# Attention over memory tokens: key loads moved from GpSimd's queue to SyncE's, with slots apart from the values

## The chip, the cores and the metric

The kernel runs on one core of one Trainium2 chip. The metric is device time in microseconds (us) of one execution, lower is better. The engines are named as in the profile: PE is TensorE (matmuls), PEld its weight loads, DVE is VectorE, ACT is ScalarE, POOL is GpSimd, SP is SyncE, which only issues DMAs. PSUM is where matmuls accumulate; SBUF is the on-chip memory from which engines read; DRAM holds inputs, outputs and scratch.

## The reference, cut to what matters

One decoder layer is computed for a prompt (256 tokens) and for 8 samples of 8 tokens (64 tokens), with the same weights: a mixer (state space and short convolution), attention over 256 memory tokens, and a retrieval layer over single-neuron experts (PEER). The change lies in the attention, 4 heads of 512:

```python
def mem_attend(xn, k, v, wq, wo):
    b, L, _ = xn.shape
    q = (xn @ wq).reshape(b, L, MEM_HEADS, MEM_HEAD_DIM)
    s = jnp.einsum('blhd,bmhd->bhlm', q, k.astype(q.dtype)).astype(jnp.float32) * (1.0 / math.sqrt(MEM_HEAD_DIM))
    p = jax.nn.softmax(s, axis=-1)
    o = jnp.einsum('bhlm,bmhd->blhd', p.astype(v.dtype), v).reshape(b, L, D_MODEL)
    return (o @ wo).astype(xn.dtype)
```

For the samples, keys and values are inputs (`cache_mem_k`, `cache_mem_v`), one set for each sample and head. For the prompt they are computed at the start of the kernel, written out as results (`p_mem_k`, `p_mem_v`), and read back here. A tile is the keys, or the values, of one sample (or of the prompt) for one head: 256 tokens x 512 numbers in fp32, 512 KB, held as 128 partitions x 1024. That makes 4 heads x (8 samples + 1 prompt) = 36 key tiles and 36 value tiles.

## The kernel before, in words

All of the work is one stream of units (class `Stream`). A unit has up to four parts: `load` (asks for a weight tile by DMA), `first` (for a key tile: the transpose on DVE, L1363), `second` (split of an fp32 tile into a high part H on ACT, L248, and a low part L on DVE, L249), and `comp` (the matmuls). `add` puts a unit into the stream; its `first` runs in program order some units later (`ahead`), and its `comp` later still, when more units of its kind are queued than `room` allows. So the code itself writes down the order of PE, ACT and DVE (`MANUAL` names these three engines). The order of requests on SP and on POOL isn't fixed by hand there: the framework's planner sorts each of these queues while it builds the program, and puts a wait ahead of each request for the slot that it fills. Later in the kernel POOL's order is fixed too, but not in the stage of the change.

In the attention stage three kinds of units alternate (list `steps`): weight units of the next head's query projection (`panel`, `w_mem_q`) or of the output projection (`w_mem_o`), key units and value units. Weight tiles (W) are 512 KB each, in four slots, asked for by SP. Key units of head h come nine to a head: eight samples, then the prompt. Value units of a head follow its keys by nine key steps and four more (`nk`, `LAG`), so that the values of head h run between the keys of head h+1; after the last key only values and weight units are left.

Key units of samples: `next_tile()` hands out a loaded tile kv, `turned` transposes it into a tile tt (three buffers), and `comp` multiplies it with the queries into pss (L1408). From that moment, the end of the transpose, the kv slot is free. Key units of the prompt: the same transpose, then the split into H and L, then psp (L1424 to L1426). When a head's scores are complete, a side job copies them (SC, L1307), gathers them by further matmuls (psm, L1314), and runs the softmax. Value units of samples: `first` only hands out the tile, and the matmuls of two tiles run together in the second one's `comp` (pso, L1448); the slots of both are free after that. Value units of the prompt: split, then po (L1466 to L1468), then the split of the result into AH and AL.

Loads before: `kv_load` appends a closure to one list, `loads`, for keys and values in the order in which they are used, and `next_load` runs the next one. All ask on POOL's queue: two DMAs of 256 KB for a sample's keys (L1129, each fills 64 partitions), four of 128 KB for the prompt's keys (L1129, 32 partitions), one of 512 KB for values (L1132). All share ten slots of one tag (`KVT`), seven in pool KV and three in pool PQ, used in turn. Eight tiles are asked for ahead of the stage; from the fourth tile on, each `next_tile` first asks for one more (`KV_AHEAD` = 5), so that five tiles of either kind are ahead.

Of the kernel before, what the change touches and what calls it, by code (L numbers as in the profile page):

```python
# [11 lines left out]
F32 = mybir.dt.float32  # L12
# [7 lines left out]
P = 128  # L20
# [5 lines left out]
NB = 8  # L26
# [15 lines left out]
PE_U, PE_B, DVE_T, ACT_H, DVE_L, POOL_L = 1.44, 1.36, 0.66, 0.6, 0.76, 1.36  # L42

HLB, GD, WA, WB = 7, 6, 3, 4
TU, AB, TTB, KVT, KV1, OB = 5, 3, 3, 10, 7, 3

R_SSD, R_BEST, R_CHOOSE, R_CHOOSE2, R_OUT = 0.7, 0.6, 0.40, 0.32, 0.29
XW, LAG = 5, 4
# [1 line left out]
Q_AHEAD, Q_ROOM, KV_AHEAD = 5, 4, 5  # L50
# [113 lines left out]
def step(ctx, tc, ins, outs, dbg=None, stop=None):  # L164
    nc = tc.nc
# [78 lines left out]
    strm = Stream(WA, g=GD, a=2)  # L244
# [869 lines left out]
        scaled_split(h[:, k], l[:, k], x[:, k], gain(g, k))  # L1114
        add_square(nrm, acc, x[:, k], k == 0)

    loads = deque()
    ready = deque()
    tiles = count()
    PQ = {}  # L1120

    def kv_load(src, blocks):
        def load():
            own = next(tiles) % KVT < KV1
            t = (KV if own else PQ)["pool"].tile([P, 1024], F32, tag="kv", bufs=KV1 if own else KVT - KV1, name="kv")
            if blocks:
                n, p = 512 // blocks, P // blocks
                for e in range(blocks):
                    nc.gpsimd.dma_start(t[p * e:p * e + p].rearrange("p (a d) -> p a d", d=n),  # L1129
                                        src[:, n * e:n * e + n].rearrange("(a p) d -> p a d", p=p))  # L1130
            else:
                nc.gpsimd.dma_start(t.rearrange("p (m d) -> p m d", m=2), src.rearrange("(m p) d -> p m d", p=P))  # L1132
            ready.append(t)
        loads.append(load)

    def next_load():
        if loads:
            loads.popleft()()

    skipped = count()  # L1140

    def next_tile():
        if next(skipped) >= NB - KV_AHEAD:
            next_load()
        return ready.popleft()

    KV = {}

# [6 lines left out]
    for c in range(8):  # L1155
        gemm(w_out[0], 256 * c, 256, AH, AL, T, lambda m, pt, c=c: evac_next(XF, 2 * c + m, pt, norm_sum(1), 2, BH, BL))
        strm.then(lambda c=c: nc.gpsimd.dma_start(x1_d[:, 2 * c:2 * c + 2], XF[:, 2 * c:2 * c + 2]))
        if c == 1:
            strm.then(open_kv)
        if 2 <= c <= 5:  # L1160
            strm.then(next_load)
            if c < 5:
                strm.then(next_load)
    if dbg is not None and "x1" in dbg:
        strm.flush()
        dump("x1", XF)
# [7 lines left out]

    def open_q():
        PQ["pool"], PQ["close"] = pool("pQ")
        next_load()
    strm.then(open_q)

    def panel(w2d, c, ah, al, evac, wide=False, need=()):  # L1180
# [44 lines left out]
    def open_tiles():  # L1225

        pq = PQ["pool"]
        PQ["sel"] = pq.tile([P, TS], F32, name="sel")
        iv = ident.rearrange("p (y u x q) -> p y u x q", y=2, u=2, q=LS)
        V.tensor_tensor(PQ["sel"].rearrange("p (x y q) -> p y x q", y=2, q=LS), iv[:, :, 0], iv[:, :, 1], ALU.add)  # L1230
        def clear(name, shape):
            t = pq.tile(shape, F32, name=name)
            S.activation(t, ident[:, 0:shape[2]].unsqueeze(1).broadcast_to(shape), AF.Copy, scale=0.0)
            return t
        PQ["half"] = clear("half", [P, 4, 32])
        for s in range(2):
# [124 lines left out]
    def turned(t, k):  # L1361
        tt = PQ["pool"].tile([P, 1024], F32, tag="tt", bufs=TTB, name="tt")
        V.transpose(tt.rearrange("p (k a i) -> p k a i", k=k, i=32), t.rearrange("p (a k j) -> p k a j", k=k, j=32))  # L1363
        return tt

    def prompt_units(src, keys, comp):

        kv_load(src, 4 if keys else 0)
        box = {}

        def unit(u):
            def first():
                if u == 0:
                    t = next_tile()
                    box["t"] = turned(t, 4) if keys else t

            def second():
                h, l = high(), low()
                split(h, l, box["t"][:, 512 * u:512 * u + 512])
                box[u] = h, l  # L1380

            def third():
                comp(u, *box.pop(u))

            return None, first, second, third, "a"

        return [unit(0), unit(1)]

    def head(h):

        st = {}

        def sample_scores(b):

            if h:
                kv_load(cache_k[0, b, :, h], 2)

            def first():
                st["k", b] = turned(next_tile(), 8)

            def comp():
                if b == 0:
                    st["ss"] = ps("pss")
                tt = st.pop(("k", b))
                for i in range(2):
                    for j in range(4):
                        k = 4 * i + j
                        PE.matmul(st["ss"][32 * j:32 * j + 32, P * (b // 2):P * (b // 2) + P], PQ["qm"][:, k * NB + b],  # L1408
                                  tt[:, P * k:P * k + P], start=b % 2 == i == 0, stop=b % 2 == i == 1)
                if b == NB - 1:  # L1410
                    strm.side(sample_softmax(st["ss"], h), 1 + h // 3)

            return [(None, first, None, comp, "a")]

        def prompt_scores(u, kh, kl):
            if u == 0:
                st["sp"] = ps("psp")
            for j in range(2):
                c = 2 * u + j
                for qb in range(2):  # L1420
                    out = st["sp"][:, TP * qb:TP * qb + TP]
                    qh, ql = (PQ[n][:, c, qb * P:qb * P + P] for n in ("qh", "ql"))
                    k0, k1 = kh[:, TP * j:TP * j + TP], kl[:, TP * j:TP * j + TP]
                    PE.matmul(out, qh, k0, start=c == qb == 0, stop=False, skip_group_check=True)  # L1424
                    PE.matmul(out, qh, k1, start=False, stop=False, skip_group_check=True)
                    PE.matmul(out, ql, k0, start=False, stop=c == 3, skip_group_check=True)  # L1426
            if u == 1:
                strm.side(prompt_softmax(st["sp"], h), 1 + h // 3)

        def sample_values(b):  # L1430

            def unit(i):
                kv_load(cache_v[0, i, :, h], 0)

                def first():
                    st["v", i] = next_tile()

                def comp():
                    if i == b:
                        return  # L1440
                    assert ("pm", h) in done
                    if b == 0:
                        st["so"] = ps("pso")
                    vs = [st.pop(("v", n)) for n in (b, i)]
                    for y, v in enumerate(vs):
                        for u in range(2):
                            g = 2 * y + u
                            PE.matmul(st["so"][32 * g:32 * g + 32], PQ["pm"][:, u * NB + b + y], v[:, 512 * u:512 * u + 512],  # L1448
                                      start=b == 0, stop=b == NB - 2)
                    if i == NB - 1:  # L1450
                        st["res"] = strm.side(sample_result(st["so"], h), 1 + h // 2)
                        done.add(("sv", h))

                return None, first, None, comp, "a"

            return [unit(b), unit(b + 1)]

        def prompt_values(u, vh, vl):
            assert ("ph", h) in done
            if u == 0:  # L1460
                st["po"] = [ps(f"po{c}") for c in range(2)]
            for j in range(4):
                out = st["po"][j // 2][:, TP * (j % 2):TP * (j % 2) + TP]
                v0, v1 = vh[:, j * P:(j + 1) * P], vl[:, j * P:(j + 1) * P]
                p0, p1 = PQ["ph"][:, u], PQ["pl"][:, u]
                PE.matmul(out, v0, p0, start=u == 0 and j % 2 == 0, stop=False, skip_group_check=True)  # L1466
                PE.matmul(out, v0, p1, start=False, stop=False, skip_group_check=True)
                PE.matmul(out, v1, p0, start=False, stop=u == 1, skip_group_check=True)  # L1468
            if u == 1:
                for c in range(2):  # L1470
                    k = 4 * h + 2 * c
                    split(AH[:, k:k + 2, 0:TP], AL[:, k:k + 2, 0:TP], st["po"][c].rearrange("p (j t) -> p j t", t=TP))
                done.add(("pv", h))

        def keys(b):
            return sample_scores(b) if b < NB else prompt_units(p_mem_k[0, 0, :, h], True, prompt_scores)

        def values(b):
            if b == NB:
                return prompt_units(p_mem_v[0, 0, :, h], False, prompt_values)  # L1480
            return sample_values(b - 1) if b % 2 else []

        return keys, values
# [451 lines left out]
    box = {}  # L1935

    turned, lowered, used = {}, {}, {}
# [364 lines left out]
```

## Time and profile before

| what | us |
|---|---|
| median of 3 runs | 3092.66 |
| lowest and highest of them | 3091.08, 3093.04 |
| the profiled execution | 3084.24 |
| its span, first to last instruction | 3082.5 |
| PE busy in the span | 3047.4 |
| DVE, ACT, POOL busy | 2269.7, 1586.2, 1347.8 |
| first transpose of a key tile, start | 1157.8 |
| last matmuls with sample values, start | 1347.9 |

The profile is one execution on the chip. A line such as "1314.39 1.25 DVE L1363 ..." in an order of time is: start in us from the span's start, duration in us, engine, line of the kernel, operation, tile written <- tiles read (buffer numbers left out), their shapes, how many instructions in a row, and in brackets how long the engine stood before it and what ended that. An engine with a q (SPq, POOLq) is its sequencer. POOL's DMA lines show how long POOL took to issue, not to transfer. In a table by windows the columns are the window, its length, the busy us of PE, PEld, DVE, ACT and POOL with their instruction counts, the granted PE clock, the busy share of the 16 DMA engines, and GB/s. A row on waits is "who <- what it waited for: us in total, times, longest".

### The profile page before, as it was taken

Reading aid. Unit: us, or ns where it says so; the run is one execution under the profiler, and the core shown is the slowest. Engines: PE = TensorE matmul, PEld = TensorE weight load, DVE = VectorE, ACT = ScalarE, POOL = GpSimd, SP = SyncE. Lnnn points to the kernel's source line nnn. Section 1 sums busy time; section 2 is a strip of 40 time slices with the busy share of each in tenths; the row PEclk is TensorE's granted clock in tenths of the full one; section 3 lists DMA queues with packets and bytes.
Section 4 is the critical chain, followed back from the end, with each engine's and each line's share of the span. In section 5 each row is a group of like instructions: output and inputs, shape, how many; then the busy total and the mean of one; then the engine's idle time right before and its main releaser. Section 6 shows DMA issues by size and latency. Waiting matters only on the chain. (4 is left out here: it accounts for less than half of the span.)

```text
span 3082.5 us, 55315 instructions
## 1 busy us (share of the span) xinstructions
PE 3047.4 (99%) x19709; PEld 2791.6 (91%) x19709; DVE 2269.7 (74%) x4478; ACT 1586.2 (51%) x3200; POOL 1347.8 (44%) x1500
## 2 busy tenths in 40 slices
PE   8999999999999999999999999999999999999998
PEld 7889999999999999889999999888888888888886
DVE  5556866666566556656778899988885888888886
ACT  5545543434454443444454444766674555555555
POOL 0011221111110002410458999988887656455553
PEclk9999999999999999999999999999999999999999
DMA  7988899899999858975966788878998999999996
GB/s 270 294 266 301 308 332 328 307 331 308 356 327 344 296 185 225 268 246 159 239 205 222 286 320 316 303 290 323 332 333 270 351 338 364 321 348 338 319 314 216
DMA packets 445321, 909.19 MB, mean 295 GB/s; under 512 B 43336, under 2 KB 252400, under 8 KB 419572
## 3 DMA queue, kind: packets, MB, share of 16 engines
q1 hardware_dynamic: 316372, 543.31, 51.5%
q0 software_dynamic: 60656, 227.34, 22.4%
q10 hardware_dynamic: 68016, 135.01, 12.8%
q8 instruction: 154, 2.52, 0.3%
q14 instruction: 123, 1.01, 0.1%
HBM read 849.44 MB, written 190.05 MB: 337 GB/s over the span
## 5 line engine op out<-in xcount | busy, mean ns | idle before, releaser
L249 DVE TENSOR_TENSOR L<-W,H 128x512 fp32r<-128x512 f32 x1312 | 900.7, 711 | 360.7 <-ACT H L248 351.4
L248 ACT ACTIVATE H<-W 128x512 fp32r<-128x512 f32 x1312 | 796.6, 628 | 684.8 <-PE acc L2170 232.2
L1979 POOL TENSOR_TENSOR L<-tt,H 128x512 fp32r<-128x512 f32 x511 | 646.4, 1296 | 59.9 <-ACT H L1976 52.7
L371 PE MATMUL pg<-AH,H 128*128 128x320 f32 x1856 | 581.7, 313 | 0.0
L373 PE MATMUL pg<-AH,L 128*128 128x320 f32 x1856 | 573.7, 309 | 0.0
L372 PE MATMUL pg<-AL,H 128*128 128x320 f32 x1856 | 573.4, 309 | 0.0
L2169 PE MATMUL acc<-L,wt 128*128 128x512 f32 x1024 | 398.7, 389 | 1.1 <-DVE L L249 1.0
L2170 PE MATMUL acc<-H,wt 128*128 128x512 f32 x1024 | 398.4, 389 | 0.0
L2168 PE MATMUL acc<-H,wt 128*128 128x512 f32 x1024 | 398.4, 389 | 0.0
L1976 ACT ACTIVATE H<-tt 128x512 fp32r<-128x512 f32 x512 | 308.6, 625 | 144.2 <-DVE tt L1967 117.5
L1967 DVE STREAM_TRANSPOSE tt<-W 128x512 f32<-128x512 f32 x512 | 337.6, 690 | 56.9 <-POOL L L1979 52.7
L1998 PE MATMUL pu<-XP,H 128*128 128x512 f32 x1035 | 371.3, 399 | 0.0
L371 PEld LDWEIGHTS pg<-AH,H 128*128 128x128 f32 x1856 | 349.0, 188 | 2.1 <-issue 0.5
L372 PEld LDWEIGHTS pg<-AL,H 128*128 128x128 f32 x1856 | 348.7, 188 | 1.8
L373 PEld LDWEIGHTS pg<-AH,L 128*128 128x128 f32 x1856 | 348.4, 188 | 0.0
L1999 PE MATMUL pu<-XP,L 128*128 128x256 f32 x1104 | 297.1, 279 | 0.2 <-POOL L L1979 0.2
L2121 POOL TENSOR_TENSOR at<-at,G 128x108 f32<-128x108 f32 x192 | 160.6, 850 | 260.5 <-DMA at<-act_d 210.8
L2005 PE MATMUL pu<-XP,L 128*128 128x256 f32 x944 | 269.4, 285 | 2.7 <-POOL L L1979 2.4
L2003 PE MATMUL pu<-XP,H 128*128 128x256 f32 x944 | 267.8, 284 | 0.0
L2004 PE MATMUL pu<-XP,H 128*128 128x256 f32 x944 | 267.0, 283 | 0.0
L1998 PEld LDWEIGHTS pu<-XP,H 128*128 128x128 f32 x1035 | 194.3, 188 | 39.9
L2169 PEld LDWEIGHTS acc<-L,wt 128*128 128x128 f32 x1024 | 192.2, 188 | 42.2 <-DVE L L249 2.4
(497 smaller groups left out, 5791.6 us busy)
## 6 DMA issues: line engine op xcount, KB each, us to landing
u_d<-in_peer_u_dram ACTq DMA_DIRECT2D x128, 1024.0 KB
W<-u_d SPq DMA_DIRECT2D x128, 1024.0 KB
W<-in_peer_v_dram SPq DMA_DIRECT2D x256, 512.0 KB
W<-in_w_in_dram SPq DMA_DIRECT2D x176, 512.0 KB
W<-in_w_out_dram SPq DMA_DIRECT2D x64, 512.0 KB
W<-in_w_mem_k_dram SPq DMA_DIRECT2D x32, 512.0 KB
W<-in_w_mem_v_dram SPq DMA_DIRECT2D x32, 512.0 KB
kv<-in_cache_mem_k_dram POOLq DMA_DIRECT2D x64, 256.0 KB
```

The lines of the kernel that those rows point to most:

```text
L248: S.activation(h, src, AF.Copy)
L249: V.tensor_tensor(l, src, h.bitcast(F32), ALU.subtract)
L371: PE.matmul(out, hv[:, j, c0:c1], ah[:, k, 0:n], start=st, stop=False)
L372: PE.matmul(out, hv[:, j, c0:c1], al[:, k, 0:n], start=False, stop=False)
L373: PE.matmul(out, lv[:, j, c0:c1], ah[:, k, 0:n], start=False, stop=sp)
L1967: V.transpose(tt.rearrange("p (k a i) -> p k a i", a=4, i=32), box["x", i].rearrange("p (a k j) -> p k a j", a=4, k=16)[:, 4 * q:4 * q + 4])
L1976: S.activation(h, src, AF.Copy)
L1979: G.tensor_tensor(l, src, h.bitcast(F32), ALU.subtract)
L1998: PE.matmul(*wide, start=k == 0, stop=False)
L2168: PE.matmul(out, th, h, start=j == 0, stop=False)
L2169: PE.matmul(out, th, l, start=False, stop=False)
L2170: PE.matmul(out, tl, h, start=False, stop=j == P - 1)
```

## The change

Three things are changed.

- Requests for keys, of samples and of the prompt, are issued by SP (`nc.sync`) in place of POOL (`nc.gpsimd`). Values stay on POOL.
- The ten slots are divided. Five (tag kk, in pool KV) are for keys; five (tag vv, two in pool KV and three in pool PQ) are for values. Until ten keys have been asked for, numbers 5 to 9 of them use the vv slots, since no value is needed yet. Values are asked for only after the tenth key.
- There are two lists of loads. `fill`, called at each `next_tile`, asks for as many keys and values as have a slot by its own account (`alive`). A key's slot counts as free at the next `next_tile` after its transpose, a sample value pair's two slots after the pair's matmuls, a prompt value's after its last matmuls.

The tiles, the transposes, the splits, the matmuls and their order on PE, ACT and DVE are as before.

```diff
-TU, AB, TTB, KVT, KV1, OB = 5, 3, 3, 10, 7, 3
+TU, AB, TTB, KVK, KVV, KV1, OB = 5, 3, 3, 5, 5, 2, 3
...
     def kv_load(src, blocks):
         def load():
-            own = next(tiles) % KVT < KV1
-            t = (KV if own else PQ)["pool"].tile([P, 1024], F32, tag="kv", bufs=KV1 if own else KVT - KV1, name="kv")
+            kind = "kk" if blocks and not KVK <= keys_out < KVK + KVV else "vv"
+            own = kind == "kk" or next(shared) % KVV < KV1
+            t = (KV if own else PQ)["pool"].tile([P, 1024], F32, tag=kind, bufs=KVK if kind == "kk" else KV1 if own else KVV - KV1,
+                                                 name="kv")
+            alive[kind] += 1
             if blocks:
                 n, p = 512 // blocks, P // blocks
                 for e in range(blocks):
-                    nc.gpsimd.dma_start(t[p * e:p * e + p].rearrange("p (a d) -> p a d", d=n),
-                                        src[:, n * e:n * e + n].rearrange("(a p) d -> p a d", p=p))
+                    nc.sync.dma_start(t[p * e:p * e + p].rearrange("p (a d) -> p a d", d=n),
+                                      src[:, n * e:n * e + n].rearrange("(a p) d -> p a d", p=p))
             else:
                 nc.gpsimd.dma_start(t.rearrange("p (m d) -> p m d", m=2), src.rearrange("(m p) d -> p m d", p=P))
-            ready.append(t)
-        loads.append(load)
...
-    def next_tile():
-        if next(skipped) >= NB - KV_AHEAD:
-            next_load()
-        return ready.popleft()
+            ready["k" if blocks else "v"].append((t, kind))
+        loads["k" if blocks else "v"].append(load)
+
+    def next_key():
+        nonlocal keys_out
+        loads["k"].popleft()()
+        keys_out += 1
+
+    def fill():
+
+        while loads["k"] and alive["vv" if KVK <= keys_out < KVK + KVV else "kk"] < (KVV if KVK <= keys_out < KVK + KVV else KVK):
+            next_key()
+        while loads["v"] and keys_out >= KVK + KVV and alive["vv"] < KVV:
+            loads["v"].popleft()()
+
+    def release(kind):
+        alive[kind] -= 1
+
+    def next_tile(kind):
+        while done_with:
+            release(done_with.popleft())
+        fill()
+        t, where = ready[kind].popleft()
+        if kind == "k":
+            done_with.append(where)
+        return t
...
                         for u in range(2):
                             g = 2 * y + u
                             PE.matmul(st["so"][32 * g:32 * g + 32], PQ["pm"][:, u * NB + b + y], v[:, 512 * u:512 * u + 512],
                                       start=b == 0, stop=b == NB - 2)
+                    release("vv")
+                    release("vv")
```

More of the change, by code (lines that the diff above doesn't have):

```diff
@@ L1115, in evac_next @@
         add_square(nrm, acc, x[:, k], k == 0)
-    loads = deque()
-    ready = deque()
-    tiles = count()
     PQ = {}
+    loads, ready = ({kind: deque() for kind in "kv"} for _ in range(2))
+    alive = dict(kk=0, vv=0)
+    shared = count()
+    keys_out = 0
+    done_with = deque()
     def kv_load(src, blocks):
         def load():
-            own = next(tiles) % KVT < KV1
-            t = (KV if own else PQ)["pool"].tile([P, 1024], F32, tag="kv", bufs=KV1 if own else KVT - KV1, name="kv")
+            kind = "kk" if blocks and not KVK <= keys_out < KVK + KVV else "vv"
[3 more added lines that the diff above has]
+            alive[kind] += 1
             if blocks:
@@ L1128, in load @@
                 for e in range(blocks):
-                    nc.gpsimd.dma_start(t[p * e:p * e + p].rearrange("p (a d) -> p a d", d=n),
-                                        src[:, n * e:n * e + n].rearrange("(a p) d -> p a d", p=p))
+                    nc.sync.dma_start(t[p * e:p * e + p].rearrange("p (a d) -> p a d", d=n),
+                                      src[:, n * e:n * e + n].rearrange("(a p) d -> p a d", p=p))
             else:
                 nc.gpsimd.dma_start(t.rearrange("p (m d) -> p m d", m=2), src.rearrange("(m p) d -> p m d", p=P))
-            ready.append(t)
-        loads.append(load)
[L1136 to L1140, printed above, removed]
-    def next_tile():
-        if next(skipped) >= NB - KV_AHEAD:
-            next_load()
-        return ready.popleft()
+            ready["k" if blocks else "v"].append((t, kind))
[19 more added lines that the diff above has]
+        return t
     KV = {}
@@ L1160, in step @@
         if 2 <= c <= 5:
-            strm.then(next_load)
+            strm.then(next_key)
             if c < 5:
-                strm.then(next_load)
+                strm.then(next_key)
     if dbg is not None and "x1" in dbg:
@@ L1176, in open_q @@
         PQ["pool"], PQ["close"] = pool("pQ")
-        next_load()
+        next_key()
     strm.then(open_q)
@@ L1373, in first @@
                 if u == 0:
-                    t = next_tile()
+                    t = next_tile("k" if keys else "v")
                     box["t"] = turned(t, 4) if keys else t
@@ L1383, in third @@
                 comp(u, *box.pop(u))
+                if u == 1:
+                    box.clear()
+                    if not keys:
+                        release("vv")
             return None, first, second, third, "a"
@@ L1398, in first @@
             def first():
-                st["k", b] = turned(next_tile(), 8)
+                st["k", b] = turned(next_tile("k"), 8)
             def comp():
@@ L1435, in first @@
                 def first():
-                    st["v", i] = next_tile()
+                    st["v", i] = next_tile("v")
                 def comp():
@@ L1449, in comp @@
                                       start=b == 0, stop=b == NB - 2)
+                    release("vv")
+                    release("vv")
                     if i == NB - 1:
```

## The prediction

> **What bounds the kernel now.** The page gives the span and TensorE (PE) at work in 3047.4 us of it, 99%, so only stretches where PE stands can be won. The change touches one stage, memory attention, from about 1157 us (first key transposed, L1363) to 1354 us. The first view is therefore who waited for whom, on PE alone, in 1150 to 1360 us.
>
> ```profile
> span 3082.5 us, 55315 instructions
> ...
> PE 3047.4 (99%) x19709; PEld 2791.6 (91%) x19709; DVE 2269.7 (74%) x4478; ACT 1586.2 (51%) x3200; POOL 1347.8 (44%) x1500
> ```
>
> ```profile
> PE psm L1314 <- ACT SC L1307: 2.5, 1, 2.5
> PE pg L1215 <- DVE AL L249: 2.0, 1, 2.0
> PE ppp L241 <- DVE AL L249: 0.7, 1, 0.7
> PE ppp L241 <- DVE SP L1301: 0.6, 1, 0.6
> PE pso L1339 <- DVE AL L249: 0.3, 1, 0.3
> ```
>
> Those are all: 2.5+2.0+0.7+0.6+0.3 = 6.1 us. That is the **ceiling** of a gain in this stage, and 0.2% of 3092.66 is 6.2 us, about what a measurement of this kernel can tell from no change. Which of the five hang on keys? The order of time on VectorE (DVE) says it for the first two; the last number of a row is idle time and what ended it.
>
> ```profile
> 1314.39 1.25 DVE L1363 STREAM_TRANSPOSE tt<-kv 128x1024 f32<-128x1024 f32 x1 [1.11 <-DMA kv<-in_cache_mem_k_dram]
> 1315.56 0.65 DVE L249 TENSOR_TENSOR L<-W,H 128x512 fp32r<-128x512 f32 x1
> 1316.13 0.68 DVE L249 TENSOR_TENSOR pl<-ppp,ph 128x512 fp32r<-128x512 f32 x1
> 1316.73 0.41 DVE L249 TENSOR_TENSOR AL<-pso,AH 128x256 fp32r<-128x256 f32 x1
> 1317.06 0.68 DVE L249 TENSOR_TENSOR L<-W,H 128x512 fp32r<-128x512 f32 x1
> 1321.61 1.25 DVE L1363 STREAM_TRANSPOSE tt<-kv 128x1024 f32<-128x1024 f32 x1 [3.88 <-DMA kv<-out_dram]
> ```
>
> DVE works in program order. The split AL at 1316.73, for which PE waits 2.0 us, stands behind a transpose that waited 1.11 us for a sample key. At 1321.61 the prompt's key tile of the last head came 3.88 us late. ScalarE (ACT) needs that transpose before it can copy the scores, and PE waits 2.52 us for the copy:
>
> ```profile
> 1323.49 0.58 ACT L1307 ACTIVATE SC<-pss 128x512 f32<-128x512 f32 x1
> ```
>
> ```profile
> 1324.12 0.96 PE L1314 MATMUL psm<-SC,half 128*32 128x128 f32 x14 [2.52 <-ACT SC L1307]
> ```
>
> The other three (1.6 us) hang on softmax work that the change leaves alone. Why was the tile late? The last of its four requests on GpSimd (POOL):
>
> ```profile
> 1311.48 0.58 POOL L1129 DMA_DIRECT2D kv<-out_dram  x1 [0.98 <-DMA kv<-in_cache_mem_k_dram]
> ```
>
> From 1311.48 to 1321.61 are 10.1 us, in a stretch with the DMA engines full. The windows (next to last number: DMA share) and the queues in 1240 to 1340 (packets, MB, share) show that most of it is POOL's own queue q0:
>
> ```profile
> 1300.00:1320.00 20.00, 17.76 (x199) 14.35 (x200) 13.83 (x24) 7.35 (x18) 6.87 (x12) 1.00 1.04 272
> 1320.00:1340.00 20.00, 17.48 (x145) 13.79 (x144) 10.78 (x21) 9.47 (x23) 7.50 (x11) 1.00 0.97 352
> ```
>
> ```profile
> q0 software_dynamic: 6303, 21.85, 76.3%
> q1 hardware_dynamic: 4048, 6.82, 25.1%
> ```
>
> **The change, part by part.** *Issue.* 80 key requests go from POOL to SyncE (SP).
>
> ```profile
> L1129 POOL DMA_DIRECT2D kv<-in_cache_mem_k_dram x64: 617/624/667, 887.4 to 1300.3; - x64
> L1129 POOLq EVENT_SEMAPHORE  x28: 17/17/43, 895.7 to 1305.9; - x28
> L1129 POOL DMA_DIRECT2D kv<-out_dram x16: 582/588/612, 1142.0 to 1311.5; - x16
> ```
>
> ```profile
> L1190 SPq DMA_DIRECT2D W<-in_w_mem_q_dram x32: 367/368/368, 1116.7 to 1261.2; - x32
> ```
>
> POOL loses 64 x 0.624 + 16 x 0.588 = 49 us, SP gains about 80 x 0.368 = 29 us. PE's waits name neither queue's issue time, so both count 0; without that cover one tile is worth 2 x (0.624-0.368) = 0.5 us.
>
> *SP's queue.* A key request now waits for a slot, and behind it stand weight loads (W). SP is not among the engines whose order is written by hand, so the planner may move requests. On POOL it did: in the code two x_d stores (L1157) precede the first key, yet the keys went out first.
>
> ```profile
> 887.41 4.94 POOL L1129 DMA_DIRECT2D kv<-in_cache_mem_k_dram  x8 [8.94 <-PE pt L241]
> 915.85 3.68 POOL L1129 DMA_DIRECT2D kv<-in_cache_mem_k_dram  x6 [23.50 <-DVE XS L1076]
> 1041.27 0.57 POOL L1157 DMA_DIRECT2D x_d<-XF  x1 [121.73 <-DVE XF L1113]
> ```
>
> What frees a weight slot is a DVE split, what frees a key slot a DVE transpose:
>
> ```profile
> SPq L1190 <- DVE L L249: 116.5, 28, 13.5
> ```
>
> One in-order engine frees both, so requests sorted by readiness hold each other up little: 0. The other end is the first rival.
>
> *Keys' lead.* Five key slots of their own: a request waits for the transpose five keys earlier. For the last prompt tile that is head 3's key 3:
>
> ```profile
> 1301.62 1.24 DVE L1363 STREAM_TRANSPOSE tt<-kv 128x1024 f32<-128x1024 f32 x1
> ```
>
> It ends at 1302.9; four requests of 0.37 follow to 1304.4, where now the fourth starts at 1311.48. With the same 10.1 us it lands by 1314.5, before DVE asks at 1317.06+0.68 = 1317.7. The next wait ahead of psm is the matmuls whose scores are copied; PE reaches psm at 1324.12-2.52 = 1321.6. The transpose would end at 1319.0, H and the score copy (0.6 each) by 1320.2. So all 2.52 go: **-2.5**, bounds -2.5 and 0 (should it land no sooner). The 1.11 us wait is for a key that has the same request time (slot of key 2) but no values ahead in its queue: I take **-1.1**, bounds -1.1 and 0.
>
> *Values' slots.* This is what the change pays. Before, ten slots served both kinds; now values have five, and once keys end, the five key slots lie idle. A value tile holds its slot until its pair's matmuls (L1448). Before, the last head's values went out far ahead:
>
> ```profile
> 1326.35 2.10 POOL L1132 DMA_DIRECT2D kv<-in_cache_mem_v_dram  x3 [3.76 <-PE pso L1448]
> 1333.92 2.11 POOL L1132 DMA_DIRECT2D kv<-in_cache_mem_v_dram  x3 [5.46 <-PE pso L1448]
> 1336.02 0.70 POOL L1132 DMA_DIRECT2D kv<-out_dram  x1
> ```
>
> ```profile
> 1343.13 1.16 ACT L248 ACTIVATE H<-kv 128x512 fp32r<-128x512 f32 x2 [2.06 <-DMA kv<-out_dram]
> ```
>
> ```profile
> 1332.56 1.92 PE L1448 MATMUL pso<-kv,pm 128*32 128x512 f32 x16
> ...
> 1339.02 1.07 PE L1448 MATMUL pso<-kv,pm 128*32 128x512 f32 x8
> ...
> 1341.97 1.06 PE L1448 MATMUL pso<-kv,pm 128*32 128x512 f32 x8
> ```
>
> Four tiles requested from 1333.92 had landed at 1343.13, 9.2 us; 0.5 MB at 352 GB/s are 1.5 us, so the first took 9.2-3x1.5 = 4.7 us. By the diff, head 3's values 0 and 1 ask when head 2's pair (4,5) is done, 1333.5; 2 and 3 after pair (6,7), 1334.5. Issued 0.7 apart, they land at about 1338.5, 1340.0, 1341.5, 1343.0. Pair (0,1) ran at 1339.02 and now at 1340.0: 1.0 late. Values 5 and 6 ask at its end (1341.0) and land at 1346.0 and 1347.5; pair (2,3) runs at 1343.0, pair (4,5) one step of 2.95 later at 1345.9, 0.1 late. Value 7 and the prompt tile ask at 1344.0 and land at 1349.0 and 1350.5, in time for the late schedule. Cost **+1.1**, in the clock of before (all of it moves with the 3.6 us won above). Bounds: 0, and with 10.1 us instead of 4.7 at both round trips 1.1 + 2 x 5.4 = +11.9. I take 1.1 since its row lies in this very stretch, when keys are through. Earlier heads' pairs lie over 10 us behind their requests: 0.
>
> **Sum**: -2.5 -1.1 +1.1 = -2.5 us. After 1354 us PE is fed as before, so it stays. Span 3082.5 to 3080.0. The profiled execution took 3084.24, 8.4 below the runs' median; the same distance gives 3092.7-2.5 = **3090.2**.
>
> **Rivals.** *SP in written order.* As written, the w_mem_o tile of units 4 and 5 stands behind the last prompt key, so it would go out at 1304.4:
>
> ```profile
> 1275.16 0.37 SPq L1190 DMA_DIRECT2D W<-in_w_mem_o_dram  x1
> ```
>
> It lands at 1314.5 and the split that reads it (about 1311) is 3 us late; two or three earlier tiles fare alike, with H and L buffers between them and PE. Price +2 to +6: 3092 to 3096. Against it: the moved requests above. Chance 0.08.
>
> *Nothing lands sooner.* The stage is DMA-bound, so a request 7 us earlier queues 7 us longer; only the tail's cost stays: 3092.7+1.1 = 3093.8. For it: share 1.04. Worse, q0's packets are 21.85/6303 = 3.5 KB and q1's 1.7 KB; if engines alternate by packet, q1 gets a third while values queue. Against it: values ask later, so q0 is empty more often. Chance 0.14. The Trainium skill ("DMA: Bandwidth & Descriptors", section "Queues, rings and completion order") says each engine goes round the queues packet by packet; the two shares above, 76.3 and 25.1, fit that. The same page ("Issuing engines are not separate DMA queues") says that issuing from several engines saves only issue time; by that rule the result is this rival's.
>
> *Slower: values' round trip decides.* In the last head each pair waits for slots freed two pairs before, 4.9 us apart. From 4.9 us of landing time on, each further us costs PE one at both round trips. At 10.1 us: -3.6+11.9 = +8.3, 3101; at 7 us about 3094.9. For it: the 10.1 row. Against it: keys' traffic is over by then. Chance 0.14, most of it near 3099.
>
> *More than the ceiling*, if a later stage falls better into step: 3086. Chance 0.06. The forecast keeps 0.58.
>
> **How the numbers follow.** Low end: the ceiling, 3092.7-6.1 = 3086.5; high end 3098.0 takes in half of the slow rival. Outside lie 0.08 below and about 0.12 above. Faster by over 0.2%: 0.06 and 0.02 of the forecast, 0.08. Slower: 0.12 of the third rival and 0.01 of the first, 0.13. Same: 0.79.
>
> **What would show it.** Right: no wait of tt on kv<-out_dram; psm without its 2.5 us; the POOL waits in 1325 to 1350 all on PE pso; a new PE wait of pso L1448 on a value DMA near 1336. Wrong: ACT's H waiting for W far more than before, with PE waiting for H (first rival); the 3.88 us wait still there (second); PE waiting over 4 us for values (third).

## The result, and the profile after

The changed kernel took 3112.85 us (median of 6 runs, 3104.57 to 3115.12) beside 3089.79 us for the kernel before on the same chip: ratio 1.0069, 95% interval 1.0057 to 1.0082. That is about 21 us **slower**; the prediction had 3090.2 (range 3086.5 to 3098.0), no change that can be measured, and gave "slower" 0.13. The profiled execution took 3104.57 us with a span of 3102.9, 20.4 more than before's 3082.5. Each profile is one execution, and both of these are at the low end of their kernel's times; what differs between them is read as what differs between the medians.

The page of the changed kernel, TensorE (PE) row. PE is busy 10.7 us longer, with the same 19709 matmuls: part of the loss is not idle time.

```profile
span 3102.9 us, 55311 instructions
...
PE 3058.1 (99%) x19709; PEld 2798.0 (90%) x19709; DVE 2271.9 (73%) x4478; ACT 1588.0 (51%) x3200; POOL 1301.5 (42%) x1420
```

Where are the 20.4 us? Three tiles of PE serve as milestones: prq at the start of memory attention, po (first and last start) and psm. The view of one tile, before and then after; the pair of times near the end of a row are the starts of its first and last matmul.

```profile
L1255 PE MATMUL prq<-ones,acc x6: 166/234/250, 1145.2 to 1145.7; 128*128 128x1 f32 x4, 128*64 128x1 f32 x2
L1466 PE MATMUL po<-ph,H x32: 278/283/386, 1264.9 to 1354.1; 128*128 128x256 f32 x32
L1314 PE MATMUL psm<-SC,half x64: 272/273/297, 1204.0 to 1324.9; 128*32 128x128 f32 x64
```

```profile
L1273 PE MATMUL prq<-ones,acc x6: 164/234/250, 1152.2 to 1152.7; 128*128 128x1 f32 x4, 128*64 128x1 f32 x2
L1490 PE MATMUL po<-ph,H x32: 278/283/561, 1271.8 to 1374.2; 128*128 128x256 f32 x32
L1332 PE MATMUL psm<-SC,half x64: 272/273/297, 1211.0 to 1339.4; 128*32 128x128 f32 x64
```

The first prq is 7.0 us late (1152.2 - 1145.2). From there to the first po nothing changes (119.7 and 119.6). From the first po to the last psm it takes 67.6 instead of 60.0: 7.6. From there to the last po 34.8 instead of 29.2: 5.6. Behind it 0.3. 7.0 - 0.1 + 7.6 + 5.6 + 0.3 = 20.4. So there are **three losses**, and the first lies ahead of the stage that the prediction looked at.

PE's waits in 800 to 1420 us of the changed kernel (total, times, longest):

```profile
PE ppp L241 <- DVE AL L249: 5.2, 1, 5.2
PE pg L371 <- ACT H L248: 4.5, 1, 4.5
PE pso L1470 <- DMA kv<-in_cache_mem_v_dram: 3.0, 3, 1.8
PE po L1490 <- ACT pm L1345: 2.0, 1, 2.0
PE psm L1332 <- ACT SC L1325: 1.0, 1, 1.0
PE pg L1233 <- DVE AL L249: 0.8, 1, 0.8
PE ppp L241 <- DVE SP L1319: 0.5, 1, 0.5
PE pso L1357 <- DVE AL L249: 0.3, 1, 0.3
```

psm's wait fell from 2.5 to 1.0 and pg's from 2.0 to 0.8, the way that the prediction had it. But 4.5 (near 948), 2.0 and 5.2 (1274 and 1284) and 3.0 (values) are new. The sum is 17.3, 11.2 above before's 6.1; most of the other 9 us are matmuls at a lower clock. The windows, one of before and then those of the changed kernel (PE's busy time and number of matmuls come first, PEclk third from the end):

```profile
940.00:960.00 20.00, 20.00 (x139) 20.00 (x138) 15.70 (x30) 12.78 (x26) 0.00 (x0) 1.00 1.07 395
```

```profile
940.00:960.00 20.00, 15.53 (x86) 15.04 (x85) 10.29 (x21) 8.54 (x18) 0.00 (x0) 0.83 1.03 364
...
950.00:955.00 5.00, 5.00 (x21) 5.00 (x20) 4.78 (x11) 4.67 (x10) 0.00 (x0) 0.52 0.94 299
...
1276.00:1277.00 1.00, 1.00 (x7) 1.00 (x6) 0.36 (x1) 0.00 (x0) 0.00 (x0) 0.50 1.03 410
...
1286.00:1290.00 4.00, 4.00 (x30) 3.46 (x29) 2.68 (x5) 1.61 (x3) 0.00 (x0) 0.58 0.67 186
```

Before, 940 to 960 held 139 matmuls; now 86. 53 x 20/139 = 7.6 us are lost there, 4.5 of them idle and some 3 in matmuls at half clock after the wait.

**First loss, near 948.** The order of time on ScalarE (ACT) and on SyncE's queue (SPq; a row's second number spans all its requests):

```profile
947.80 0.63 ACT L248 ACTIVATE H<-W 128x512 fp32r<-128x512 f32 x1 [8.25 <-DMA W<-in_w_out_dram]
```

```profile
913.97 8.44 SPq L1134 DMA_DIRECT2D kv<-in_cache_mem_k_dram  x8
923.04 2.72 SPq L347 DMA_DIRECT2D W<-in_w_out_dram  x2
926.50 6.45 SPq L1134 DMA_DIRECT2D kv<-in_cache_mem_k_dram  x5
936.19 22.70 SPq L347 DMA_DIRECT2D W<-in_w_out_dram  x9
```

ACT waits 8.25 us for a weight tile of the GEMM with w_out. Head 0's keys had gone out in a bunch on the same queue, with few weight requests in between (a few per cent of the records are missing).

**Second loss, 1264 to 1285.** SyncE's queue, then VectorE (DVE), ACT and PE:

```profile
1264.07 1.92 SPq L1134 DMA_DIRECT2D kv<-out_dram  x4
1268.79 0.39 SPq L1208 DMA_DIRECT2D W<-in_w_mem_q_dram  x1
1272.49 1.27 SPq L1134 DMA_DIRECT2D kv<-in_cache_mem_k_dram  x2
1273.85 0.56 SPq L1208 DMA_DIRECT2D W<-in_w_mem_q_dram  x1
```

```profile
1263.97 0.65 DVE L249 TENSOR_TENSOR L<-W,H 128x512 fp32r<-128x512 f32 x1
1269.41 0.69 DVE L249 TENSOR_TENSOR L<-W,H 128x512 fp32r<-128x512 f32 x1 [4.79 <-ACT H L248]
1270.02 1.29 DVE L249 TENSOR_TENSOR L<-kv,H 128x512 fp32r<-128x512 f32 x2
1271.22 1.24 DVE L1381 STREAM_TRANSPOSE tt<-kv 128x1024 f32<-128x1024 f32 x1
...
1283.37 0.69 DVE L249 TENSOR_TENSOR L<-W,H 128x512 fp32r<-128x512 f32 x1 [7.00 <-ACT H L248]
1283.97 1.28 DVE L249 TENSOR_TENSOR AL<-po,AH 128x512 fp32r<-128x512 f32 x2
```

```profile
1268.75 0.63 ACT L248 ACTIVATE H<-W 128x512 fp32r<-128x512 f32 x1 [6.19 <-DMA W<-in_w_mem_q_dram]
...
1282.70 0.63 ACT L248 ACTIVATE H<-W 128x512 fp32r<-128x512 f32 x1 [7.56 <-DMA W<-in_w_mem_q_dram]
```

```profile
1284.71 1.11 PE L241 MATMUL ppp<-ident,SP 128*128 128x128 f32 x4 [5.15 <-DVE AL L249]
```

Read it as a **loop**. The split at 1263.97 frees a weight slot at 1264.6. Its request goes out at 1273.85, 9.2 us later, because a key request stands ahead of it on SyncE (1272.49) and waits for the transpose that ends at 1272.46. That transpose stands on DVE behind a split that waited 4.79 us for H, and H waited 6.19 us for an earlier weight tile. So late weights delay the transpose, the transpose holds the key request, and the key request holds the next weights. The kernel before had no such hold; its rows of DVE and SPq:

```profile
1262.89 0.64 DVE L249 TENSOR_TENSOR L<-W,H 128x512 fp32r<-128x512 f32 x1
```

```profile
1263.56 11.97 SPq L1190 DMA_DIRECT2D W<-in_w_mem_o_dram  x3
```

The split ends at 1263.53 and the request starts at 1263.56. Worked out like this for the nine weight tiles that land in 1235 to 1295 (request minus the end of the split that freed the slot four tiles earlier), the hold is 0.0 us before and 9.0 on average after; from free slot to landing it is 11.0 and 21.3 us.

**Third loss, the values' tail.** PE and GpSimd (POOL) at the end of the stage, after:

```profile
1355.47 1.05 PE L1470 MATMUL pso<-kv,pm 128*32 128x512 f32 x4 [1.84 <-DMA kv<-in_cache_mem_v_dram]
1357.06 1.05 PE L1470 MATMUL pso<-kv,pm 128*32 128x512 f32 x4 [0.54 <-DMA kv<-in_cache_mem_v_dram]
...
1360.00 1.06 PE L1470 MATMUL pso<-kv,pm 128*32 128x512 f32 x8
```

```profile
1340.90 0.72 POOL L1137 DMA_DIRECT2D kv<-in_cache_mem_v_dram  x1 [6.18 <-PE pso L1470]
1341.62 0.72 POOL L1137 DMA_DIRECT2D kv<-out_dram  x1
1349.58 3.61 POOL L1137 DMA_DIRECT2D kv<-in_cache_mem_v_dram  x5 [7.24 <-DVE L L249]
```

The last head's first five values all go out from 1349.58, 4 us before PE is ready for the first pair (1355.47 - 1.84 = 1353.6). The semaphores in the trace tell which request is which. The first of the five waits for the split of head 2's prompt value (until 1349.3), and only head 3's second pair needs it. Values 0 and 1 are the second and third request. By the kernel's account they have slots when head 2's pair (4,5) ends, at 1348.2, but they stand behind the first request, go out at 1350.30 and 1351.03, and land at 1355.34 and 1357.02. A pair whose second value is late also runs in two pieces of 1.05 us, where the whole pair takes 1.06.

### The profile page after: what moved, and what is told of

Same layout as the page of the kernel before. It is cut to its first block, busy times and chain, and to the rows that moved or that the text cites. A ratio compares the mean times of both kernels' runs of the same rounds, so it can differ in the third digit from the quotient of the medians.

```text
span 3102.9 us, 55311 instructions
## 1 busy us (share of the span) xinstructions
PE 3058.1 (99%) x19709; PEld 2798.0 (90%) x19709; DVE 2271.9 (73%) x4478; ACT 1588.0 (51%) x3200; POOL 1301.5 (42%) x1420
## 3 DMA queue, kind: packets, MB, share of 16 engines
q8 instruction: 154, 2.52, 0.3%
## 4 chain that ended last, share of the span: by engine, by line
PE 80%; DMA 6%; DVE 5%; issue 4%; POOL 3%; ACT 1%; SPq 0%; DVEq 0%; ACTq 0%; POOLq 0%
PE pg L371 11%; PE pg L373 11%; PE pg L372 11%; PE pu L2022 8%; PE acc L2193 6%; PE acc L2194 5%; PE acc L2192 5%; PE pu L2023 4%; POOL L L2003 2%; PE pgate L1925 2%; PE pg L318 2%; PE pg L319 2%; PE pg L320 2%; DMA gv<-in_peer_v_dram,EV 1%; PE pu L2029 1%
```

## The experiments

Two theories to begin with. **Q**: the keys stand in SyncE's queue ahead of the weights. **S**: the divided slots and the new order of requests did it. All ratios are to the kernel before on the same chip.

**Keys back on GpSimd** (keys_gpsimd). Nothing else differs from the changed kernel.

```diff
-                    nc.sync.dma_start(t[p * e:p * e + p]...
+                    nc.gpsimd.dma_start(t[p * e:p * e + p]...
```

> The changed kernel with one word altered: the key requests go out on GpSimd again; slots, filling order and releases stay as changed. Theory Q (the keys stand in SyncE's queue ahead of the weights): both weight waits go, PE pg <- ACT H near 943 (the offset against before grows by 7.7 us there) and the two stalls of 1272 to 1290 (10.3 us), and what is left is the values' tail, 2 to 3 us: about 3112.9 - 18 = 3095 us, 3090 to 3098. Theory S (the divided slots and the order of requests did it): the stalls stay, 3105 or more.

3092.5 us, ratio 1.0003 (0.9992 to 1.0014): by the ratios (1.0069 and 1.0003) 20 us won back by one word. PE's waits:

```profile
PE pso L1470 <- DMA kv<-in_cache_mem_v_dram: 3.3, 3, 1.8
PE ppp L241 <- DVE AL L249: 0.7, 1, 0.7
PE ppp L241 <- DVE SP L1319: 0.6, 1, 0.6
PE pso L1357 <- ACT O L1353: 0.4, 1, 0.4
```

No wait for weights is left, and the hold of weights is 0.0 again. Theory S falls as the main cause. psm's and pg's waits of before (2.5 and 2.0) are gone from the list too, but only pg's with its cause: DVE no longer waits for a sample key. For the last prompt key it still stands, nearly as long as before (3.88):

```profile
1318.26 1.25 DVE L1381 STREAM_TRANSPOSE tt<-kv 128x1024 f32<-128x1024 f32 x1 [3.53 <-DMA kv<-out_dram]
```

PE just comes to psm later here, since it stood 1.77 and 1.02 us for values at 1313 to 1316.

**First eight keys on GpSimd, later ones on SyncE** (early_gpsimd), **and the reverse** (late_gpsimd).

```diff
+                    (nc.gpsimd if keys_out < NB else nc.sync).dma_start(...   # early_gpsimd
+                    (nc.sync if keys_out < NB else nc.gpsimd).dma_start(...   # late_gpsimd
```

> The changed kernel with only the first eight keys (those of head 0, asked for while the GEMM with w_out runs) on GpSimd, all later keys on SyncE. Theory Q: the stall near 943 goes and the one at 1272 to 1290 stays: 3112.9 - 7.7 = about 3105. Theory S: no change, 3113. If the two stalls are one chain (the first sets the step of the second), both go or the second changes: 3095 or some other value than 3105.

> The changed kernel with the first eight keys (head 0) on SyncE and all later ones on GpSimd: the other half of the run in which the first eight went out on GpSimd (3105.0). If the two weight stalls are separate, each with its own price, only the one near 943 is left: 3092.5 + 7.7 to 8.5 = about 3100.5, and PE's offset against before is 7 to 9 us from 950 to 1330. If one of them needs the other, this comes out near 3092 or near 3110.

3105.0 us, ratio 1.0039 (1.0025 to 1.0053), and 3099.69 us, ratio 1.0029 (1.0015 to 1.0044). By the ratios that is about 11 and 8 us above keys_gpsimd, together 19, and the changed kernel is 20 above it. Each interval is some 4 us to either side; within that, what the early and the late keys cost on SyncE is separate, and adds. The milestones agree (table below): prq is late in late_gpsimd and on time in early_gpsimd.

**The kernel before with its keys on SyncE** (before_sync), and **the changed kernel with each key request cut in two** (halves).

```diff
-                    nc.gpsimd.dma_start(t[p * e:p * e + p]...        # before_sync
+                    nc.sync.dma_start(t[p * e:p * e + p]...
```

```diff
+                    m = to.shape[1] // 2                             # halves
+                    for f in range(2):
+                        nc.sync.dma_start(to[:, m * f:m * f + m], at[:, m * f:m * f + m])
```

> The kernel before with one word altered: the key requests go out on SyncE; the ten shared slots, their order and everything else as before. Theory Q: SyncE's queue alone makes it slow, 3100 or more, with ACT's H waiting for W and PE for H. Theory S: the queue costs nothing, 3088 to 3092.

> The changed kernel with each key request cut into two of half the bytes (same rows, same packets, still on SyncE): sample keys four requests a tile, the prompt's eight. The trace of the changed kernel never shows more than seven SyncE requests in flight when another goes out, and in the stretch 915 to 941 each goes out within 0.1 us of an earlier one's landing. If that limit on requests in flight is what delays the weights (Q1), half the bytes in each place cost much more: over 3120. If it is the bytes ahead of them in the queue (Q2), only the issue time is added, 80 x 0.37 us beside other work: 3112 to 3116.

before_sync: 3102.65 us, ratio 1.0026 (1.0010 to 1.0042). Its profiled execution has the first loss (prq at 1154.8) and hardly any tail loss (30.3). The queue alone makes the old kernel slow. It doesn't make the loop: with the ten shared slots the hold of weights in 1235 to 1295 is 1.3 us on average, not 9.0. What grows between po and psm (65.2) is psm's wait, from 2.5 to 5.6 us, since DVE stands 8.4 us for the last prompt key. So the second loss needs both, the queue and the requests as the divided slots let them be written. halves: 3112.51 us, ratio 1.0064 (1.0050 to 1.0079), no slower than 3112.85. So the number of requests in flight isn't the price. With half the key bytes ahead of it a weight request spends less time under way (8.8 us at the median in 905 to 945, against 11.5), but it waits that much longer to go out: from free slot to landing it is 21.8 us in 1235 to 1295, against 21.3.

**Prompt keys on GpSimd as well** (prompt_gpsimd), for the four requests at 1264.07 look like the culprit.

```diff
+                    (nc.gpsimd if keys_out < NB or blocks == 4 else nc.sync).dma_start(...
```

> The changed kernel with the first eight keys and the four prompt key tiles on GpSimd; the 24 sample key tiles of heads 1 to 3 stay on SyncE. In the changed kernel the weight tile asked for at 1268.47, which lands at 1282.28 and for which PE stands, went out behind the prompt tile's four requests (1263.76 to 1265.37). Theory P (it is these four): the stall at 1272 to 1290 goes, about 3105.0 - 10 = 3095. Theory B (it is all keys' bytes ahead of the weights, two thirds of which stay): the stall stays or shrinks a little, 3100 to 3105.

3102.36 us, ratio 1.0034 (1.0020 to 1.0049). Theory P falls: with the sample keys alone on SyncE, the stretch from po to psm is as long as ever (70.4).

**SyncE in written order** (written).

```diff
     def open_kv():
+        written.enter_context(tc.manual_schedule(engines={ET.SP}))
...
     def residual_in():
+        written.close()
```

> The changed kernel with SyncE's requests held to the order in which the kernel writes them, from the opening of the key slots to the end of memory attention. In the changed kernel 14 of the first 16 key requests go out between 913 and 933 with only two weight requests among them, though the code writes four weight tiles between each two key tiles there. If it is this bunching that starves the weights near 943, the stall there goes: 3105 or less, by what the later stages make of it. If the keys' bytes on that queue cost the same wherever they stand: 3112.

3099.69 us, ratio 1.0022 (1.0006 to 1.0038). The first loss is gone (prq at 1145.5), and SyncE's queue says why: in the written order the first keys go out at 1061, not 913.

```profile
906.04 155.05 SPq L347 DMA_DIRECT2D W<-in_w_out_dram  x46
1061.19 3.65 SPq L1134 DMA_DIRECT2D kv<-in_cache_mem_k_dram  x4
```

The planner had moved them some 150 us ahead of their written place, in front of weights that PE needed. The other losses stay: PE's 4.0 us wait of ppp on AL is still there, and the hold of weights is 9.5 us. From po to psm only 2.9 us are lost, though, so the hold alone does not say how much PE loses.

**Slots counted free two keys later** (delayed), on top of early_gpsimd; **one key later** is tried below.

```diff
-        while done_with:
+        while len(done_with) > 2:
             release(done_with.popleft())
```

> As the run with the first eight keys on GpSimd (3105.0), but a key slot counts as free two keys later, so that its request is written when the transpose that frees it lies two steps back. In that run and in the changed kernel the weight requests of 1225 to 1277 went out 9 us on average after their slot was free (in the kernel before 0.0), each right behind a key request that had waited. Theory L (the key request waits for a transpose that stands on VectorE behind a split of late weights: a loop through the queue): with the transposes done, the hold falls below 4 us and the stall at 1272 to 1290 shrinks by most of its 10 us, about 3096 to 3098, unless the shorter lead of the keys (three slots) makes a wait of its own. Theory B (the keys' bytes ahead of the weights): hold and stall stay, 3105.

3096.79 us, ratio 1.0021 (1.0011 to 1.0031), as theory L had it. The weights' hold falls from 9.8 us (early_gpsimd) to 2.4, and the second loss is gone:

```profile
L1490 PE MATMUL po<-ph,H x32: 278/283/386, 1265.0 to 1357.9; 128*128 128x256 f32 x32
L1332 PE MATMUL psm<-SC,half x64: 272/273/297, 1204.2 to 1321.8; 128*32 128x128 f32 x64
```

From the first po to the last psm it is 56.8 us, 3.2 **less** than before's 60.0. That is the gain which the prediction had worked out (2.5 + 1.1), seen at last with nothing on top of it. The key's fourth request goes out 6.4 us earlier than before (1305.1 and 1311.5), the tile is 3.1 us earlier (its transpose starts at 1318.54 and 1321.61). Then the tail takes 36.1 instead of 29.2.

**Values in the key slots once the last key is out** (tail_slots, on top of keys_gpsimd), and **four key and six value slots** (tail_46, on top of tail_slots). The diff is cut to the part that asks; a tile's slot is then freed under the kind it was taken from.

```diff
+        while loads["v"] and keys_out == 4 * NB + 4 and alive["kk"] < KVK:
+            loads["v"].popleft()("kk")
```

> Keys on GpSimd as in the run that came out at 3092.5, and when the last key has been asked for, values may also take the five key slots. If the tail (PE pso waiting 3.3 us for values, the offset against before growing from -1.2 at 1325 to 2.8 at 1375) comes from values having five slots and not from the queue, it goes: 3092.5 - 3 to 4 = about 3089, just below the kernel before. If later stages give it back, or the round trip was set by bandwidth: 3092.5.

> As the run with keys on GpSimd and key slots open to values at the end (3086.1), with four key slots and six value slots instead of five and five. Its largest PE wait left is 3.6 us for a value near 1317. If that is for want of value slots, it goes and the time falls by up to 3.6 us, to 3083. If it comes from GpSimd's requests in flight (seven at nearly every issue there), nothing changes, 3086; if keys now come late, 3088 to 3092.

tail_slots: 3086.13 us, ratio 0.9984 (0.9968 to 1.0000), the fastest kernel of this study, but not clear of the kernel before: the interval reaches 1. Its tail is before's again, 29.2. In its profile (of an execution 8.6 us above its median) PE waits 3.6 us for a value at 1317 instead. tail_46: 3091.93 us, ratio 1.0010 (1.0000 to 1.0020): with four slots keys come late (DVE stands 6.64 us for one).

**Both remedies** (delayed_tail2: delayed, with values in the key slots at the end), and the same with **one key of delay** (delayed_tail1).

> The run with slots counted free two keys later (3096.8) and, when the last key has been asked for, values in the key slots too. In that run PE's offset against before is 0.1 at 1300, -3.1 at 1325 (the prompt key's tile in time, as the prediction had it) and 3.5 at 1350 (the values' tail). If the two parts add, the tail's 6.6 us go: 3096.8 - 6.6 = about 3090, and from before's side 3090 - 3.1 = 3087 if nothing comes later. If the tail is set by the transfers and not by slots: 3094 to 3097.

> The same with one key of delay instead of two: keys have a lead of four slots instead of three, and a request is written one step after the transpose that frees its slot. Theory L: if one step is enough, the weights' hold stays below 4 us and the time is that of two keys of delay or a little less; if the transpose has mostly not run by then, the hold grows towards 9 us and the stall at 1272 to 1290 comes back in part, 2 to 8 us slower than with two.

delayed_tail2: 3094.46 us, ratio 1.0007 (0.9994 to 1.0021), short of the 3087 to 3090 expected: the parts don't add. The tail is 29.2, but DVE now stands for a sample key ahead of it:

```profile
1319.54 1.25 DVE L1385 STREAM_TRANSPOSE tt<-kv 128x1024 f32<-128x1024 f32 x1 [8.03 <-DMA kv<-in_cache_mem_k_dram]
```

That key's two requests took 16.1 and 17.7 us; in delayed the same two took 10.9 and 11.5. The extra values come to mind, but they can't be the whole of it: the two key requests before these took 17.3 and 18.0 us (10.6 and 11.2 in delayed), and went out at 1288.55 and 1289.20, while up to 1306 both kernels ask for the same values. Why these keys are slow stays open. delayed_tail1: 3099.39 us, ratio 1.0031 (1.0016 to 1.0046), with a hold of 5.8 us. So one step of delay leaves more of the hold than two (3.4 in delayed_tail2), but the stall at 1272 to 1290 comes back only as 2.5 us of ppp. What its profile shows above all is a late key again: psm waits 8.9 us for the last prompt key.

```profile
1334.47 1.25 DVE L1385 STREAM_TRANSPOSE tt<-kv 128x1024 f32<-128x1024 f32 x1 [10.22 <-DMA kv<-out_dram]
```

With before_sync these are three profiles with keys on SyncE in which PE's longest wait of this stage hangs on a late key (5.6, 8.1 and 8.9 us). tail_46 has the like with keys on GpSimd and four slots (6.5 us), so it isn't the queue's alone. It is a price beside the hold, and no run isolates it.

The milestones, one profiled execution each (us), worked out as above; "rest" is from the last po to the end of the span, "hold" that of the weight tiles that land in 1235 to 1295, on average:

| kernel | first prq | prq to po | po to psm | psm to last po | rest | hold |
|---|---|---|---|---|---|---|
| before | 1145.2 | 119.7 | 60.0 | 29.2 | 1728.4 | 0.0 |
| after | 1152.2 | 119.6 | 67.6 | 34.8 | 1728.7 | 9.0 |
| keys_gpsimd | 1143.4 | 119.7 | 60.6 | 33.2 | 1732.7 | 0.0 |
| early_gpsimd | 1144.6 | 119.8 | 69.8 | 36.9 | 1732.5 | 9.8 |
| late_gpsimd | 1154.7 | 119.6 | 63.5 | 33.5 | 1734.4 | 0.0 |
| before_sync | 1154.8 | 119.7 | 65.2 | 30.3 | 1733.2 | 1.3 |
| halves | 1157.1 | 121.9 | 67.6 | 35.5 | 1727.7 | 13.9 |
| prompt_gpsimd | 1142.9 | 119.7 | 70.4 | 36.3 | 1728.7 | 7.4 |
| written | 1145.5 | 119.7 | 62.9 | 34.7 | 1739.7 | 9.5 |
| delayed | 1145.3 | 119.7 | 56.8 | 36.1 | 1737.0 | 2.4 |
| tail_slots | 1144.9 | 119.6 | 63.6 | 29.2 | 1735.7 | 0.0 |
| tail_46 | 1147.0 | 119.6 | 67.6 | 29.2 | 1730.4 | 0.0 |
| delayed_tail2 | 1143.5 | 119.6 | 66.0 | 29.2 | 1732.2 | 3.4 |
| delayed_tail1 | 1147.0 | 119.7 | 71.8 | 31.0 | 1730.3 | 5.8 |

No edit touches the rest, yet it goes from 1727.7 to 1739.7, and the first column goes from 1142.9 to 1147.0 among the kernels without the first loss. So only large steps are to be read, and the columns say where a kernel loses better than one execution's total does. That late_gpsimd and tail_slots lose 3.5 us in the third column, by waits of pso, was not followed further.

## Why the prediction was wrong

**The step that failed** is "SP's queue", priced 0: "One in-order engine frees both, so requests sorted by readiness hold each other up little". Both halves of the sentence misled.

*Sorted by readiness.* The prediction showed that the planner moves requests: key requests at 887 and 915 ahead of a store written before them. It took this for good news. On GpSimd it cost nothing: no weights stand behind the keys there, and early_gpsimd, which asks for them on GpSimd from 886 to 921, has its prq on time. The same move on SyncE put head 0's keys in front of the GEMM's weights and cost 7 us (first loss: gone in written, in early_gpsimd and in keys_gpsimd). The stage looked at, from 1157 us, left out the very stretch in which these requests go out, and the ceiling with it.

*One engine frees both.* That DVE frees weight slots and key slots alike doesn't keep their requests apart, it ties them together: DVE stands when weights are late, and then key requests stand in front of weight requests. The loop cost 7.6 us net between po and psm. It needs a key request that is written as soon as its transpose is: two steps later, the loop is broken (delayed), and with the ten shared slots it hardly forms (before_sync, hold 1.3).

**The gains** (-2.5 and -1.1) were right as a mechanism: delayed shows 3.2 us of the 3.6. In the changed kernel the weights' loop lies on top of them. The transfer time in them was too short: the prediction gave the prompt key 10.1 us, and its four requests took 9 to 14 us in delayed and 12 to 15 in the changed kernel, so the tile is still late (DVE stands 1.9 and 2.3 us for it). And the -1.1 does not come from the new queue, as the prediction had it: DVE's wait for the sample key goes in keys_gpsimd too, where keys and values share GpSimd's queue, and stays in before_sync, with the keys on SyncE (1.1).

**The values' tail** (+1.1) was the right mechanism too, with its size wrong: 5.6 us. The round trip was well chosen (4.7 us; values 0 and 1 took 5.0 and 6.0), and so were the slots: the requests at 1340.90 and 1341.62 follow head 2's pair (2,3), as they should by the diff. What it lacked is the order on GpSimd's queue. By the prediction head 3's values 0 and 1 ask as soon as pair (4,5) is done, and land 5.0 and 6.5 us after that; in the changed kernel they stood behind a request that waited for the prompt value's split, and landed 7.2 and 8.9 us after. A request that waits held others here too, on the other queue. Beside 3.0 us of idle time, two pairs run in two pieces, 1 us more each.

**The rivals.** The first had the hold itself, a weight request behind a key request that waits for its slot, and its sign: in 1200 to 1300 ACT's H waits 32.9 us for W tiles, 14.7 before. It tied this to the written order, priced it at 2 to 6 us and gave it 0.08; the planner's order holds the weights as well, and puts the first loss on top, which the written order doesn't have. "Nothing lands sooner" is half right: in delayed a request 6.4 us earlier brought the tile 3.1 us earlier, and in keys_gpsimd its sign, DVE's long wait for the prompt key, is still there (3.53). The shares 76.3 and 25.1, which the prediction took as a fit for packets that go out in turn, count what each queue was given (6303 and 4048 packets), so they neither show nor contradict that. The Trainium skill ("DMA: Bandwidth & Descriptors", section "Issuing engines are not separate DMA queues") says that issuing from several engines saves only issue time. As a rule for this kernel's time it fails: 3092.5 us with keys on GpSimd and 3112.85 with keys on SyncE (ratios 1.0003 and 1.0069), everything else alike. The measurement decides. What made the difference is what stands behind a request that waits. "Values' round trip decides" is the third loss, about a quarter of the whole, though by requests that went out late more than by slow transfers.

## What to carry to other kernels

Before moving a request to another engine's queue, list what stands behind it there, over the whole stretch in which it can go out and in the order that the planner makes, and ask what each request waits for. A request that waits for a slot should stand behind nothing urgent: give such requests a queue without urgent work, or write them late enough that the slot is free when they come up. Look for loops above all: if the slot is freed by an engine that waits for what stands behind the request, a small delay feeds itself.

## What the runs showed of the hardware

- **The clock after a wait.** After 4.47 us of idle time the granted clock was 0.52 in 950 to 955, and after 5.15 us it was 0.58 in 1286 to 1290; before, a wait of 2.52 us at 1321.6 left it at 1.00. Some 3 us beside the 4.5 idle were paid so at the first loss. The Trainium skill ("TensorE: Matmul & The Clock Gate", section "What's actually happening") has the clock halved after an idle window of about 3.4 us; these three agree. A wait of only 2.0 us, up to 1274.71, was followed by a clock of 0.50 in 1276 to 1277, and for two us more. The clock record of the trace shows what the slow stretches have in common: they are 948.00 to 954.82, 1275.67 to 1279.09 and 1282.50 to 1289.33, that is 6.83, 3.41 and 6.83 us long, and all six ends lie on one grid of 3.41 us. So the length of a wait alone doesn't decide; where it falls on the grid seems to count as well. How much of a step must be idle isn't shown: the step ahead of 1275.67 held the 2.0 us.
- **Requests in flight.** When a request went out in 850 to 1370 us, at most seven earlier ones of the same engine had not landed: SyncE had up to 6 before and 7 after (33 times), GpSimd 7 before (26 times) and 4 after. This is not shown to be a limit of the chip. In the trace each engine's requests carry eight semaphores (SyncE's 100 and 102 to 108, GpSimd's 111 to 118), and whenever seven were under way, the next one went out only after the last request with its own semaphore had landed. By halves, the count was not what cost time.
- **Half a pair costs a whole one.** Four of the eight value matmuls take 1.05 us by themselves and all eight 1.06: a value that comes late costs PE 1 us beside the wait.
